# Layer A of a two-layer decoder trunk: order of the transposes and loads of x, the queue of the late loads, a fifth gate buffer, wider spreads, one block turned by TensorE

## The chip, the cores and the metric

The kernel runs on one core of one Trainium2 chip. The metric is device time in microseconds of one execution. The time before is 1515.4 us, the median of three runs (1513.81 to 1519.61). One execution was also recorded by the hardware profiler; it took 1514.66 us by its own count, and its span in the profile is 1512.9 us.

Engines are named as the profile names them: PE (TensorE matmuls), PEld (its weight loads), DVE (VectorE), ACT (ScalarE), POOL (GpSimd) and SP (the sync engine, which here starts transfers). A name with q at its end (SPq) is that engine's queue of instructions.

## The reference

Input `x` is 2048 rows of 1024 floats. Two layers follow each other. Only the first, layer A, is touched by the change:

```
h = rmsnorm(x, norm_g);  u = h @ w_in            # 1024 -> 2 x 1536
xb, gate = u[..., :1536], u[..., 1536:]
xb = causal_depthwise_conv(xb, conv_w, conv_b)   # 4 taps
r = sigmoid(xb_blocks @ wr + br);  i = sigmoid(xb_blocks @ wi + bi)   # 16 blocks of 96
log_a = -8 * r * softplus(-lam);   a = exp(log_a)
b = sqrt(-expm1(2 * log_a)) * (i * xb)
hs = linear recurrence h[s] = a[s] * h[s-1] + b[s]
x = x + (hs * silu(gate)) @ w_out                # 1536 -> 1024
```

Then K and V are made once from the new stream, and layer B is a sliding-window attention with 16 heads. All is float32 by the reference.

## The kernel before, in words

Every float32 operand of a product is split into two float16 parts, high and low, after it is scaled by a power of two. A product is then three float16 products (high-high, high-low, low-high: `PASSES`), added up in one PSUM bank. The power of two comes from the operand's largest magnitude: DVE takes maxima over each partition, `f2_turn` turns that column into a row with PE, `f2_round` takes the row's maximum and cuts it to a power of two on a small diagonal, and `f2_back` multiplies that by ones, which spreads the value over 128 partitions. This sequence is called a spread here (lines 231 to 249, `floor2_steps` from line 404).

Layer A works on units. The 2048 rows are 4 chunks of 512, the 1536 channels are 4 triples of 3 x 128; unit u is triple u // 4 at chunk u % 4, 16 units in all. For each unit PE makes the x-branch product `pu` (three banks, 72 matmuls of 512 columns), the gate product `pg` (72 more), and, while the next unit's `pu` runs, the small block product `pr` of the unit before. A unit's `pr` needs the convolution's result `xc`, its parts `hl` and a shared tile `b3` that is gathered with three small copies on SP (line 713). ACT, DVE and POOL carry the convolution, the sigmoids, the recurrence and the product with SiLU; POOL starts the store of the result to `yD` in DRAM (line 837). The SiLU's output lies in a ring of four buffers `gs`; a buffer is free when its store has landed.

The products need x normalized, split and transposed (`xnT`). Chunk 0 has four blocks of 128 rows: `first_norm` (line 897) makes the parts and `first_turn` (line 910) turns them, by PE with a copy out of PSUM for the blocks in `BY_PE`, and otherwise by a DMA transpose on SP (`flip`, line 330). `proj_first` (line 576) lets unit 0's first product run in groups of blocks (`FIRST`), as they come. Chunks 1 to 3 go through `ring_loads` and `norm_block` (three buffers in, three out) and `norm_flip`, which transposes both parts of a block in one DMA. The loads of these blocks and the transposes are both on SP.

Weights: triple 0 is prepared by `first_weights`, `first_others` and `first_gates`; triples 1 to 3 by `prep(g)` (line 535), which begins at a unit chosen by `PREP_AT` and loads through `Fetch` (three buffers `st`, started on SP). `w_out` (line 1120) loads the output weights twice, once for their maximum and once to split them. The first two output blocks of 128 rows follow directly behind unit 15 (`out_parts`, `out_products`), the others are written in plain order after that, with layer B's weight preparation between them.

The order of the instructions on each engine is fixed when the kernel is built. Each piece of work is a generator that names the engine and an estimated duration; `Plan` is a list scheduler that always takes the piece that can begin first by these estimates, with 30 ns per rank added as a handicap (`WEIGHT`, `RANKA`, `FIRST_RANK`). On the chip the engines run this order with semaphores, whatever the estimates were. `landing` estimates when a load arrives and keeps `plan.dma`, the time at which the loads issued so far are through.

Of the kernel before, what the change touches and what calls it, by code (L numbers as in the profile page):

```python
# [14 lines left out]
BF16 = mybir.dt.bfloat16  # L15
# [6 lines left out]
P = 128  # L22
# [44 lines left out]
RANKA = (1, 3, 1, 4, 2, 6, 1, 5, 6, 4, 10, 6, 4, 0)  # L67
FIRST_RANK = (2, 1, 5, 4, 3, 6, 5)
X_RING = (0, 1, 4)
# [116 lines left out]
def trunk(ctx, tc, x, wA, gw, par, gains, woA, wkv, wB, woB, vec, alib, out):  # L186
# [48 lines left out]
    def f2_round(tp, n):  # L235
        m1 = xp.tile([n, 1], F32, tag="f2m", name=uniq("f2m"), bufs=2)
        dve.tensor_reduce(m1, tp, AX.X, ALU.max)
        m2 = xp.tile([n, 1], F32, tag="f2n", name=uniq("f2n"), bufs=2)
        dve.tensor_scalar(m2, m1, 1e-30, None, ALU.max)
        m3 = xp.tile([n, 1], F32, tag="f2o", name=uniq("f2o"), bufs=2)  # L240
        dve.tensor_scalar(m3.bitcast(U32), m2.bitcast(U32), 0x7F800000, None, ALU.bitwise_and)
        dg = xp.tile([n, n], BF16, tag="f2d", name=uniq("f2d"), bufs=2)
        dve.tensor_scalar(dg, id32[:n, :n], m3, None, ALU.mult)
        return dg

    def f2_back(dg, n):
        bp = pst([P, n], F32, "tp", uniq("f2b"), TP_A)
        pe.matmul(bp, ones_b[:n, :], dg, start=True, stop=True)
        return bp
# [123 lines left out]
    def landing(kb):  # L373
# [3 lines left out]
        return t - plan.now  # L377

    def take_p1(tag, shape, dt=F32):
        f = yield from take(tag)  # L380
        return f, p1.tile(shape, dt, tag=tag, name=uniq(tag), bufs=BUFS[tag])

    class Fetch:


        def __init__(self, shape, src, rank):
            self.landed = flag()
            plan.go(self.steps(shape, src), rank)

        def steps(self, shape, src):  # L390
# [3 lines left out]
            nc.sync.dma_start(self.t, src)  # L394
            yield None, landing(P * shape[-1] * (shape[1] if len(shape) > 2 else 1) / 256)
            self.landed.set()
# [7 lines left out]
    def floor2_steps(mx, n, keep, slack=300):  # L404
        lock = yield from take("f2")
        free = yield from take("tp")
        if slack:
            yield None, slack
        yield PE_, 160
# [7 lines left out]
        yield PE_, 300  # L417
# [43 lines left out]

    def split_gates_steps(W, load, pw, rank):
        st = load.t
        yield DVE_, 200, 1
# [6 lines left out]
        for i in range(2):  # L471
            yield from split_steps(
                st[:, i * GCOLS : (i + 1) * GCOLS], sc, w[:, 0, i], w[:, 1, i], flag(), lo[i], 690, rank
            )
        W["gt"], W["pg"] = w, pw
        yield lo[1]
        load.free.set()
        W["gates"].set()
# [56 lines left out]
    def prep(g):  # L535
        W = WS[g]
        rank = RANKA[9]
        yield unit_f[4 * (g - 1) + PREP_AT[g - 1]]
        st = [Fetch([P, 4, 384], wsrc(g, 0, h), rank) for h in range(2)]
        sg = Fetch([P, 2 * GCOLS], gw[g], rank)  # L540
        m = col("m", 2)
# [5 lines left out]
        yield from split_part_steps(0, W, st, pw[:, 0:1], rank)  # L547
        st = [Fetch([P, 4, 384], wsrc(g, 1, h), rank) for h in range(2)]
        yield DVE_, 900, 1
        scales_x(g, W)  # L550
        yield from split_gates_steps(W, sg, pw[:, 1:2], rank)
        m = col("m")
# [281 lines left out]
    def store(un, j, t, gs):  # L834
# [5 lines left out]
        )  # L840
        yield None, 2600
        yield y_f[t][c]
# [17 lines left out]
    xfree = [flag() for _ in range(NB - 4)]  # L860
    hlfree = [flag() for _ in range(NB - 4)]
    x0free = [flag() for _ in range(CH // P)]
    par_f, decay_f = flag(), flag()
    w0_f, w0_st, w0_lo, px_f = [flag() for _ in range(4)], [], [flag() for _ in range(KD)], flag()

# [7 lines left out]
    def first_loads():  # L873
# [36 lines left out]
    def first_turn(b, w, src, fl):  # L910
        dest = xnV[0][:, w, :, b * P : (b + 1) * P]
        if b not in BY_PE:
            yield SP_, 1900
            flip(src, dest)
            yield None, 2500
        else:
# [3 lines left out]
            for k in range(KD):  # L920
                pe.transpose(tp[:, k], src[:, k * P : (k + 1) * P], id16)
            if w == 0:
# [21 lines left out]
    def first_weights():  # L944
# [14 lines left out]
        free = yield from take("tp")  # L959
        yield PE_, 300  # L960
        tot = pst([P, 1], F32, "tp", uniq("tot"), TP_A)
        pe.matmul(tot, ones, m0, start=True, stop=True)
        yield DVE_, 800, 1
        t = col("tot")
# [14 lines left out]
        for k in range(KD):  # L979
            if k < HI_DVE:  # L980
                yield DVE_, 320, 1
                dve.tensor_scalar(w[:, 0, k], w0_st[k // 4][:, k % 4], gs[:, k : k + 1], None, ALU.mult)
# [31 lines left out]
    def first_others(st):  # L1014
        W = WS[0]
        sg = Fetch([P, 2 * GCOLS], gw[0], FIRST_RANK[1])
        m = col("m", 2)
        yield from part_max_steps(st, m[:, 0:1])
        yield from gates_max_steps(sg, m[:, 1:2])
        pw = col("pw1", 2)  # L1020
        yield from floor2_steps(m, 2, pw)
        plan.go(first_gates(sg, pw), FIRST_RANK[3])
        yield from split_part_steps(1, W, st, pw[:, 0:1], FIRST_RANK[1])

    def first_gates(sg, pw):
        W = WS[0]
        yield from split_gates_steps(W, sg, pw[:, 1:2], FIRST_RANK[3])
        yield W["set1"]
        yield W["x"]
        yield DVE_, 180, 1  # L1030
        scales_g(W)
# [37 lines left out]
    def ring_loads():  # L1069
        for p in range(NB - 4):  # L1070
# [1068 lines left out]
```

## Time and profile before

| | before |
|---|---|
| median of three runs | 1515.4 us |
| profiled execution, its own time | 1514.66 us |
| its span | 1512.9 us |
| PE busy | 1485.0 us, 98% |
| DVE busy | 1015.9 us, 67% |
| ACT busy | 881.9 us, 58% |
| POOL busy | 412.4 us, 27% |
| mean granted clock of PE | 0.998 |

The table's shares are means over the span. Unit 0's first product begins at 13.48 us, unit 1 at 60.23 us, unit 15's gate product ends near 610 us, the first output product begins at 617.28 us; layer B's main part runs from about 870 us to the end. In a row of the timeline the first two numbers are start and length in us, "x8" is the number of instructions merged, and the bracket gives the idle time of the engine just before and what ended it. "issue" as a releaser means that the profile shows none.

### The profile page before, as it was taken

The page shows a single profiled execution, that of the slowest core. Times are in us where ns is not written, and L with a number is a line of the kernel's source. Part 1 is how long each engine was busy: PE and PEld are TensorE (multiplying, and loading weights), DVE is VectorE, ACT ScalarE, POOL GpSimd, SP SyncE. Part 2 cuts the span into 40 slices and gives each one's busy share as a digit, 9 for nine tenths or more (in the row PEclk, how much of TensorE's full clock was granted, in tenths as well). Part 3 has the DMA queues.
Part 4 walks back from the last instruction along what each step waited for, and adds up shares of the span by engine and source line. Part 5 has one row for each costly group of instructions (what it writes and reads, how often), then busy time and mean ns, then how long its engine had stood idle before and what let it go on. Part 6 is the DMA issues. An engine that isn't in the chain of part 4 may idle for free.

```text
span 1512.9 us, 23171 instructions
## 1 busy us (share of the span) xinstructions
PE 1485.0 (98%) x8572; PEld 734.4 (49%) x8572; DVE 1015.9 (67%) x2230; ACT 881.9 (58%) x1777; POOL 412.4 (27%) x548
## 2 busy tenths in 40 slices
PE   5999999999999999899999999999999999999998
PEld 4444444444444444344444455555555555555554
DVE  7877778778777766974147357656666665665686
ACT  5778667667666766601026157656665655655663
POOL 1232111111122111100000044444444444444531
PEclk9999999999999999999999999999999999999999
DMA  7863122022043313796338432444544444445531
GB/s 218 208 140 102 31 81 68 27 81 69 26 138 125 96 34 118 249 325 245 128 138 311 139 91 32 104 99 96 105 99 90 101 90 102 86 102 102 105 71 43
DMA packets 232210, 174.67 MB, mean 115 GB/s; under 512 B 194720, under 2 KB 205216, under 8 KB 232096
## 3 DMA queue, kind: packets, MB, share of 16 engines
q1 hardware_dynamic: 225808, 152.19, 38.2%
q0 software_dynamic: 6144, 20.98, 4.2%
q8 instruction: 67, 1.10, 0.3%
q14 instruction: 47, 0.39, 0.1%
q10 hardware_dynamic: 144, 0.01, 0.0%
HBM read 92.93 MB, written 29.36 MB: 81 GB/s over the span
## 4 chain that ended last, share of the span: by engine, by line
PE 94%; DMA 2%; DVE 2%; ACT 1%; issue 1%; SPq 0%; DVEq 0%; ACTq 0%
PE pm L286 35%; PE po L286 18%; PE pu L286 16%; PE pg L286 15%; PE pr L286 5%; PE s L286 3%; DMA xs<-in_x_dram 1%; DMA xnT<-in_wB_dram 0%; DMA xnT<-ri 0%; DVE wo L435 0%; PE tp L1697 0%; DMA qT<-qy 0%; DVE h L816 0%; DVE xnT L1194 0%; ACT ri L903 0%
## 5 line engine op out<-in xcount | busy, mean ns | idle before, releaser
L286 PEld LDWEIGHTS <-w 128*128 128x128 f16 x2448 | 234.3, 99 | 274.5 <-issue 10.0
L286 PE MATMUL pm<-wq,xT 128*128 128x512 f16 x1536 | 339.2, 379 | 0.0
L286 PEld LDWEIGHTS <-xT 128*128 128x128 f16 x1920 | 186.3, 98 | 177.3
L286 PE MATMUL pu<-xnT,w 128*128 128x512 f16 (+2 forms) x1296 | 261.1, 360 | 7.4 <-issue 3.2
L286 PE MATMUL po<-wo,xnT 128*128 128x512 f16 x1152 | 249.7, 379 | 4.2 <-DVE wo L435 2.4
L286 PE MATMUL pg<-xnT,w 128*128 128x512 f16 x1152 | 252.0, 379 | 0.0
L286 PEld LDWEIGHTS <-xnT 128*128 128x128 f16 x1152 | 112.5, 98 | 140.1 <-issue 5.2
L286 PE MATMUL pm<-xnT,yT 128*128 128x512 f16 x768 | 174.1, 379 | 0.3 <-ACT yT L1703 0.3
L694 DVE SCALAR_TENSOR_TENSOR xc<-u,cwS,xc 128x512 f32<-128x512 f32 x144 | 110.5, 781 | 52.4 <-ACT xc L690 49.7
L1909 ACT ACTIVATE sq<-sq,bi,ssc 128x128 f32<-128x128 f32 x256 | 124.0, 488 | 5.9 <-DVE bi L1906 5.6
L286 PEld LDWEIGHTS <-yT 128*128 128x128 f16 x768 | 73.1, 98 | 82.1 <-ACT yT L1703 0.4
L311 ACT ACTIVATE xnT<-xnT,sy 128x1536 f16<-128x1536 f32 x14 | 22.0, 1571 | 128.8 <-PE po L286 128.8
L1882 ACT COPY sq<-s 128x256 f32<-128x256 f32 x128 | 39.1, 383 | 96.5 <-PE s L286 96.3
L704 POOL TENSOR_TENSOR hl<-xc,hl 128x512 f16<-128x512 f32 x32 | 43.3, 1361 | 159.9 <-ACT hl L699 155.6
L675 ACT COPY u<-pu 128x512 f32<-128x512 f32 x48 | 27.8, 584 | 87.9 <-PE pu L286 87.7
L765 ACT ACTIVATE ri<-pr,pr,rsc 128x512 f32<-128x512 f32 x96 | 69.2, 779 | 5.2 <-PE pr L286 5.0
L837 POOL DMA_DIRECT2D yD<-gs x48 | 36.8, 767 | 119.1 <-DVE gs L827 118.8
L1283 DVE SCALAR_TENSOR_TENSOR xnT<-po,cA,xnT 128x512 f32<-128x512 f32 x28 | 20.8, 748 | 72.0 <-PE po L286 72.0
L1884 DVE COPY_PREDICATED sq<-mask,s 128x256 f32<-128x256 int32 x128 | 48.3, 437 | 28.0 <-ACT sq L1882 27.9
L286 PE MATMUL pr<-hl,gw 128*128 128x512 f16 x288 | 65.2, 379 | 0.0
L1893 DVE CUSTOM_DVE_ANT_0 sq<-sq,al 128x128 f32<-128x128 f32 x256 | 63.8, 297 | 0.0
L1837 POOL TENSOR_TENSOR rq<-qva,mhalf 128x16 f32<-128x16 f32 x16 | 49.6, 3100 | 44.6 <-DVE qva L1834 32.8
(277 smaller groups left out, 2193.3 us busy)
## 6 DMA issues: line engine op xcount, KB each, us to landing
xnT<-in_wB_dram SPq DMA_DIRECT2D x32, 512.0 KB, 6.1
yD<-gs POOLq DMA_DIRECT2D x48, 256.0 KB, 2.7
st<-in_woA_dram SPq DMA_DIRECT2D x24, 512.0 KB, 4.0
xnT<-yD SPq DMA_DIRECT2D x16, 768.0 KB, 5.2
st<-in_wA_dram SPq DMA_DIRECT2D x13, 768.0 KB, 6.2
xs<-in_x_dram SPq DMA_DIRECT2D x16, 512.0 KB, 4.3
xnT<-in_x_dram SPq DMA_DIRECT2D x16, 512.0 KB, 4.9
x1D<-xnT POOLq DMA_DIRECT2D x16, 512.0 KB, 4.2
```

Of the source, the lines that this page charges most:

```text
L286: lastmm[0] = pe.matmul(o, lhsT, rhs, start=start, stop=stop, skip_group_check=True)
L311: act.activation(hi, src, AF.Copy, scale=scale)
L675: act.copy(u[:, 3:], o)
L694: dve.scalar_tensor_tensor(xc, u[:, d : d + CH], cw[:, j, d : d + 1], xc, ALU.mult, ALU.add)
L704: (pool if j in LO_POOL else dve).tensor_tensor(hl[:, 1], xc, hl[:, 0], ALU.subtract)
L765: act.activation(v, o[j], AF.Sigmoid, bias=pr[:, t0 + j, 5 + w : 6 + w], scale=W["rsc"])
L837: pool.dma_start(yD[4 * c : 4 * c + 4, :, t, :].rearrange("b p n -> p b n"), gs.rearrange("p (b n) -> p b n", n=P),)
L1837: pool.tensor_tensor(rq, qva, mhalf, ALU.pow)
L1882: act.copy(sl, o[:, :, P:])
L1884: dve.copy_predicated(sl, mask.unsqueeze(1).to_broadcast([P, 2, P]), o[:, :, 0:P])
L1893: dve.tensor_tensor_reduce(s[:, h], s[:, h], al[:, i * P : (i + 1) * P], 1.0, -3.4e38, ALU.add, ALU.max, m)
L1909: act.activation(s[:, h], s[:, h], AF.Exp, bias=d["bi"][:, h : h + 1], scale=ssc[:, h : h + 1], accum_out=d["lsum"][:, h : h + 1],)
```

## The change

- `BY_PE = (0,)`: block 1 of chunk 0 is transposed by DMA as blocks 2 and 3 are; only block 0 is turned by PE. `FIRST = ((0, 2), (2, 4))`: the first product runs over two blocks at a time instead of one, two and one.
- `HI_DVE = 4`: DVE makes four of the first eight high weight parts instead of two, ACT the other four.
- The gate weights of triple 0 are loaded in `first_loads`, in two halves into two `gs` buffers, and are no longer a `Fetch` that waits for an `st` buffer.
- `ring_loads`: the load of block p (p >= 4) waits until the transpose of the last block of the chunk before has been issued.
- The plan's estimates of a transpose are smaller, plus the time until the loads issued before it are through (`behind_loads`).
- `Fetch` starts its loads on POOL by default; SP is kept for triples 0 and 1.
- `PREP_AT`: triples 1 and 2 begin a unit later, the output weights a unit earlier.
- `gs` has five buffers.
- The diagonal of a spread is a fixed tile of 128 partitions, zero outside the corner, and the spreading matmul runs over 128 partitions instead of n.
- New ranks. In particular the recurrence of units 14 and 15 gets `RANKA[13]` = 10 added, where it was 0.

```
-PREP_AT = (1, 1, 0, 3)
-FIRST = ((0, 1), (1, 3), (3, 4))
+PREP_AT = (2, 2, 0, 2)
+FIRST = ((0, 2), (2, 4))
...
-BY_PE = (0, 1)
-HI_DVE = 2
+BY_PE = (0,)
+HI_DVE = 4
+OUT_ACT = 0
...
-RANKA = (1, 3, 1, 4, 2, 6, 1, 5, 6, 4, 10, 6, 4, 0)
-FIRST_RANK = (2, 1, 5, 4, 3, 6, 5)
+RANKA = (2, 3, 1, 4, 1, 0, 0, 5, 4, 4, 10, 6, 3, 10)
+FIRST_RANK = (1, 0, 2, 2, 0, 6, 6)
...
+    diag = [cp.tile([P, 4], BF16, name=f"diag{i}") for i in range(2)]
+    for t in diag:
+        pool.memset(t, 0.0)
...
-        dg = xp.tile([n, n], BF16, tag="f2d", name=uniq("f2d"), bufs=2)
-        dve.tensor_scalar(dg, id32[:n, :n], m3, None, ALU.mult)
-        return dg
+        cnt[0] += 1
+        dg = diag[cnt[0] % 2]
+        dve.tensor_scalar(dg[:n, :n], id32[:n, :n], m3, None, ALU.mult)
+        return dg[:, :n]
...
-        pe.matmul(bp, ones_b[:n, :], dg, start=True, stop=True)
+        pe.matmul(bp, ones_b, dg, start=True, stop=True)
...
-    BUFS = dict(W=4, st=3, mm=MM_A, tp=TP_A, u=3, xc=4, hl=4, b3=2, gs=4, ri0=4, ri1=4, q=3, h=2, gw=2, f2=1)
+    BUFS = dict(W=4, st=3, mm=MM_A, tp=TP_A, u=3, xc=4, hl=4, b3=2, gs=5, ri0=4, ri1=4, q=3, h=2, gw=2, f2=1)
...
+    def behind_loads():
+
+        return max(plan.dma - max(plan.now, plan.free[SP_]), 0)
...
-            yield SP_, 450
+            yield queue, 450 if queue == SP_ else 750
             self.t = p1.tile(shape, F32, tag="st", name=uniq("st"), bufs=BUFS["st"])
-            nc.sync.dma_start(self.t, src)
+            (nc.sync if queue == SP_ else pool).dma_start(self.t, src)
...
+        queue = SP_ if g == 1 else POOL_
+        st = [Fetch([P, 4, 384], wsrc(g, 0, h), rank, queue) for h in range(2)]
+        sg = Fetch([P, 2 * GCOLS], gw[g], rank, queue)
...
-        plan.go(first_others([st3, Fetch([P, 4, 384], wsrc(0, 1, 1), 0)]), FIRST_RANK[1])
+        st = [st3, Fetch([P, 4, 384], wsrc(0, 1, 1), 0, SP_)]
+        for i in range(2):
+            f, t = yield from take_p1("gs", [P, CH])
+            yield SP_, 500
+            nc.sync.dma_start(t[:, 0:GCOLS], gw[0, :, i * GCOLS : (i + 1) * GCOLS])
+            plan.go(arrive(240, g0_f[i]), 0)
+            g0.append(t[:, 0:GCOLS])
+            g0_free.append(f)
+        plan.go(first_others(st), FIRST_RANK[1])
...
         if b not in BY_PE:
-            yield SP_, 1900
+            yield SP_, 1300 + behind_loads()
             flip(src, dest)
-            yield None, 2500
+            yield None, 2000
...
-        sg = Fetch([P, 2 * GCOLS], gw[0], FIRST_RANK[1])
...
+        mg = col("mg", 2)
+        for i in range(2):
+            yield g0_f[i]
+            yield DVE_, 640
+            dve.tensor_reduce(mg[:, i : i + 1], g0[i], AX.X, ALU.max, apply_absolute_value=True)
+        yield DVE_, 160
+        dve.tensor_reduce(m[:, 1:2], mg, AX.X, ALU.max)
...
                 yield xfree[p - 3]
+            if p >= 4:
+                yield turned_f[(p - 4) // 4 * 4 + 3]
             yield SP_, 450
...
-        yield SP_, 2000
+        yield SP_, 1400 + behind_loads()
         flip(t, xnV[c].rearrange("p w k n -> p (w k) n")[:, :, b * P : (b + 1) * P])
-        yield None, 3000
+        turned_f[p].set()
+        yield None, 2100
```

The halves of the gate weights reach `split_gates_steps` as two tiles with two flags to free them; other estimates in the plan change by a few tens of nanoseconds.

More of the change, by code (lines that the diff above doesn't have):

```diff
@@ L383, in trunk, with __init__, steps @@
     class Fetch:
-        def __init__(self, shape, src, rank):
+        def __init__(self, shape, src, rank, queue=POOL_):
             self.landed = flag()
-            plan.go(self.steps(shape, src), rank)
-        def steps(self, shape, src):
+            plan.go(self.steps(shape, src, queue), rank)
+        def steps(self, shape, src, queue):
             self.free = yield from take("st")
-            yield SP_, 450
+            yield queue, 450 if queue == SP_ else 750
             self.t = p1.tile(shape, F32, tag="st", name=uniq("st"), bufs=BUFS["st"])
-            nc.sync.dma_start(self.t, src)
+            (nc.sync if queue == SP_ else pool).dma_start(self.t, src)
             yield None, landing(P * shape[-1] * (shape[1] if len(shape) > 2 else 1) / 256)
@@ L408, in floor2_steps @@
             yield None, slack
-        yield PE_, 160
+        yield PE_, 110
         tp = f2_turn(mx, n)
@@ L416, in floor2_steps @@
             yield None, slack
-        yield PE_, 300
+        yield PE_, 40
         bp = f2_back(dg, n)
@@ L460, in split_part_steps, with split_gates_steps @@
             st[h].free.set()
-    def split_gates_steps(W, load, pw, rank):
-        st = load.t
+    def split_gates_steps(W, st, frees, pw, rank):
         yield DVE_, 200, 1
@@ L476, in split_gates_steps @@
         yield lo[1]
-        load.free.set()
+        for f in frees:
+            f.set()
         W["gates"].set()
@@ L538, in prep @@
         yield unit_f[4 * (g - 1) + PREP_AT[g - 1]]
-        st = [Fetch([P, 4, 384], wsrc(g, 0, h), rank) for h in range(2)]
-        sg = Fetch([P, 2 * GCOLS], gw[g], rank)
+        queue = SP_ if g == 1 else POOL_
+        st = [Fetch([P, 4, 384], wsrc(g, 0, h), rank, queue) for h in range(2)]
+        sg = Fetch([P, 2 * GCOLS], gw[g], rank, queue)
         m = col("m", 2)
@@ L547, in prep @@
         yield from split_part_steps(0, W, st, pw[:, 0:1], rank)
-        st = [Fetch([P, 4, 384], wsrc(g, 1, h), rank) for h in range(2)]
+        st = [Fetch([P, 4, 384], wsrc(g, 1, h), rank, queue) for h in range(2)]
         yield DVE_, 900, 1
         scales_x(g, W)
-        yield from split_gates_steps(W, sg, pw[:, 1:2], rank)
+        yield from split_gates_steps(W, [sg.t[:, i * GCOLS : (i + 1) * GCOLS] for i in range(2)], [sg.free], pw[:, 1:2], rank)
         m = col("m")
@@ L840, in store @@
         )
-        yield None, 2600
+        yield None, 3200
         yield y_f[t][c]
@@ L861, in trunk @@
     hlfree = [flag() for _ in range(NB - 4)]
+    turned_f = [flag() for _ in range(NB - 4)]
     x0free = [flag() for _ in range(CH // P)]
     par_f, decay_f = flag(), flag()
+    g0, g0_f, g0_free = [], [flag() for _ in range(2)], []
     w0_f, w0_st, w0_lo, px_f = [flag() for _ in range(4)], [], [flag() for _ in range(KD)], flag()
@@ L959, in first_weights @@
         free = yield from take("tp")
-        yield PE_, 300
+        yield PE_, 450
         tot = pst([P, 1], F32, "tp", uniq("tot"), TP_A)
         pe.matmul(tot, ones, m0, start=True, stop=True)
-        yield DVE_, 800, 1
+        yield DVE_, 850, 1
         t = col("tot")
@@ L1015, in first_others, with first_gates @@
         W = WS[0]
-        sg = Fetch([P, 2 * GCOLS], gw[0], FIRST_RANK[1])
         m = col("m", 2)
         yield from part_max_steps(st, m[:, 0:1])
-        yield from gates_max_steps(sg, m[:, 1:2])
+        mg = col("mg", 2)
[5 more added lines that the diff above has]
+        dve.tensor_reduce(m[:, 1:2], mg, AX.X, ALU.max)
         pw = col("pw1", 2)
         yield from floor2_steps(m, 2, pw)
-        plan.go(first_gates(sg, pw), FIRST_RANK[3])
+        plan.go(first_gates(pw), FIRST_RANK[3])
         yield from split_part_steps(1, W, st, pw[:, 0:1], FIRST_RANK[1])
-    def first_gates(sg, pw):
+    def first_gates(pw):
         W = WS[0]
-        yield from split_gates_steps(W, sg, pw[:, 1:2], FIRST_RANK[3])
+        yield from split_gates_steps(W, g0, g0_free, pw[:, 1:2], FIRST_RANK[3])
         yield W["set1"]
```

6 lines of the change are left out of this document (3 added, 3 removed).

## The prediction

> **What bounds the kernel now.** I read the span on the page, then the table of stretches, then the timeline of TensorE (PE) and of the SP queue where PE stands still. The columns of the table are length, then busy us (instructions) of PE, weight loads, VectorE (DVE), ScalarE (ACT), GpSimd (POOL), then granted clock, DMA share, GB/s.
>
> ```profile
> span 1512.9 us, 23171 instructions
> ```
> ```profile
> 0.00:13.50 13.50, 2.67 (x19) 2.07 (x20) 7.42 (x17) 7.58 (x10) 3.26 (x15) 1.00 0.89 318
> 13.50:24.40 10.90, 7.84 (x84) 6.68 (x85) 10.48 (x21) 7.40 (x12) 1.06 (x3) 1.00 0.81 200
> 24.40:32.00 7.60, 6.31 (x37) 4.35 (x36) 4.38 (x8) 2.24 (x4) 0.74 (x2) 0.55 0.63 157
> 41.30:60.20 18.90, 15.77 (x74) 6.87 (x71) 16.26 (x54) 14.82 (x22) 4.66 (x11) 1.00 1.01 224
> 97.20:573.20 476.00, 476.00 (x2353) 212.44 (x2352) 368.50 (x564) 325.88 (x470) 94.33 (x175) 1.00 0.26 77
> 573.20:617.30 44.10, 42.21 (x220) 18.67 (x219) 29.34 (x44) 30.82 (x40) 8.05 (x12) 1.00 0.42 130
> 617.30:640.20 22.90, 20.54 (x94) 9.12 (x94) 21.95 (x29) 17.02 (x21) 0.00 (x0) 1.00 0.79 288
> ```
>
> From 97.2 to 573.2 us PE is never idle and no edit removes a product, so that stretch can only stay or get worse. What can be won lies in two places. The first is everything before unit 1's products begin at 60.23: the two products of unit 0 are twice a 15.54 us stretch, yet they end at 57.08 and a gap of 3.15 follows.
>
> ```profile
> 57.08 3.15 issue
> 81.65 15.54 PE pg L286 x72
> 60.23 5.34 PE pu L286 x24
> ```
>
> The second is the end of layer A, where PE waits 1.89 us for a PSUM bank that the last SiLU frees, and 0.84 and 1.51 us for the low parts of the output weights.
>
> ```profile
> 616.54 0.69 ACT L755 ACTIVATE gs<-pg,gsc 128x512 f32<-128x512 f32 x1 [4.68 <-DMA yD<-gs]
> 617.28 12.68 PE L286 MATMUL po<-wo,xnT 128*128 128x512 f16 x58 [1.89 <-ACT gs L755]
> 618.00 1.53 SPq L394 DMA_DIRECT2D st<-in_woA_dram  x2
> 630.80 0.81 PE L286 MATMUL po<-wo,xnT 128*128 128x512 f16 x3 [0.84 <-DVE wo L435]
> 633.12 7.07 PE L286 MATMUL po<-wo,xnT 128*128 128x512 f16 x32 [1.51 <-DVE wo L435]
> ```
>
> **The change part by part: the first 40 us.** Block 1 of x is no longer turned by PE, and the first product now takes blocks 0 and 1 together, so it cannot begin before block 1's high part has come through a DMA transpose. The loads ahead of that transpose end here:
>
> ```profile
> 15.50:17.40 1.90, 1.90 (x20) 1.90 (x19) 1.83 (x4) 1.90 (x4) 0.00 (x0) 1.00 1.04 388
> 17.40:19.40 2.00, 1.99 (x31) 1.75 (x29) 1.93 (x3) 2.00 (x4) 0.73 (x2) 1.00 0.07 25
> 20.20 0.34 SPq L394 DMA_DIRECT2D st<-in_gw_dram  x1
> 20.63 4.45 SPq L332 DMA_TRANSPOSE xnT<-ri  x2
> 26.46 2.10 PE L286 MATMUL pu<-xnT,w 128*128 128x256 f16 x9 [1.29 <-DMA xnT<-ri]
> 28.56 3.50 PE L286 MATMUL pu<-xnT,w 128*128 128x256 f16 x18
> 32.10 2.14 PE L286 MATMUL pu<-xnT,w 128*128 128x256 f16 x18
> ```
> ```profile
> L332 SPq DMA_TRANSPOSE xnT<-xs x12: 1791/3484/4560, 41.7 to 118.7; - x12
> L332 SPq DMA_TRANSPOSE xnT<-ri x4: 1241/1293/3011, 20.6 to 30.9; - x4
> ```
>
> The unit's gate weights (480 KB, 0.49 MB) are now loaded with the others, at 388 GB/s 1.3 us more, so the loads end at 17.4 + 1.3 = 18.7. A transpose costs SP 1.24 us and its data serve PE 1.4 us after the issue ends (20.63 + 4.45 = 25.08, PE goes on at 26.46). First product: 18.7 + 1.24 + 1.4 = 21.3, where it was 13.48. The remaining five transposes at 1.27 bring the last at 27.7, or about 29.5 if one load of a later block stays between them; PE then still has the second pair of blocks to do, so this lies beside it. (The 13.48 is no loss by itself: half of the old PE time up to 26.46 is waiting.)
>
> From 21.3 PE has 15.5 us of product, the maxima's small matmuls (three spreads of two, at 0.10 each by a row further down) and the clock. The old run was granted 0.55 between 24.4 and 32.0: from 26.46 to 32.0 eighteen matmuls take 3.50 us where the next eighteen take 2.14. The new kernel idles from 11.5 to 21.3, so I charge the same spell, 5.5 us at half clock = 2.7 us; bounds 0 (the clock in the rows stood at 1.00 at 13.5 after an idle start) and 7.6 x 0.45 = 3.4. Sum: 21.3 + 15.5 + 0.6 + 2.7 = 40.1 for the first gate product, 1.0 before the old one (41.15, the row below).
>
> ```profile
> 41.15 2.75 PE L286 MATMUL pg<-xnT,w 128*128 128x512 f16 x12
> 54.01 0.52 SPq L867 DMA_DIRECT2D xs<-in_x_dram  x1
> 54.58 3.51 SPq L332 DMA_TRANSPOSE xnT<-xs  x1
> 50.93 1.28 DVE L1096 SCALAR_TENSOR_TENSOR xs<-xs,r 128x1024 f16<-128x1024 f32 x1 [0.29 <-ACT xs L1094]
> ```
>
> The Trainium skill has a rule for this clock ("TensorE: Matmul & The Clock Gate", Part 1): PE idle for a window falls to half rate, and about 3.4 us of steady work lift it. Taking 3.4 instead of the 5.5 of the trace, the loss would be 1.7 and the time 1.0 us better; the spell in the rows is longer, so the rows decide.
>
> The gate product's weights must not be late for 40.1. Their maxima stood behind the gate weights: DVE idled 3.2 of the 7.6 us from 24.4 (waiting for that load, then for PE's turns), and with the load issued before the transposes this goes. The other shifts are small: two more high parts on DVE (0.37 each), a copy of 0.68 less; ACT has two high parts and a 0.99 copy less. I cost them at nothing; DVE is 96% busy from 13.5 to 24.4, so without cover it is 0.1 to 0.7 us.
>
> **The gap at 57.08.** Unit 1 needs chunk 1 of x. Its last low part was done at 52.2, but the transpose was issued at 54.58 behind a load and the three transposes before it, each slowed to 3.3 to 3.8 us with a load ahead of it. New: loads of later blocks wait until the chunk's four transposes are issued. A transpose of this size with nothing ahead is the row's minimum, 1.79: ready at 52.2 + 1.8 + 1.4 to 2.0 = 55.4 to 56.0 even if DVE is no earlier. PE arrives at 40.1 + 15.7 = 55.8. So unit 1 starts at about 55.8: **4.4 us saved**, at most 7.1 (no half clock and DVE earlier), at least 0.
>
> What is queued next is unit 0's small gate product, at 55.8 + 5.3 = 61.1. The convolution that feeds it had its last copy to the shared tile issued at 61.84, landing 1.9 later, 63.7. It must come 2.6 us earlier; the 3.2 us of DVE idle pay for that, barely.
>
> ```profile
> 59.91 1.93 SPq L713 DMA_DIRECT2D b<-hl  x3
> DMA to landing us min/median/max: 1.9/1.9/8.0
> ```
>
> **The end of layer A.** The last SiLU waited for the fourth-last gate buffer, whose store was issued at 610.26 and landed; with five buffers it needs the one stored at 606.69, 3.6 us earlier.
>
> ```profile
> 606.69 0.78 POOL L837 DMA_DIRECT2D yD<-gs  x1 [5.36 <-DVE gs L827]
> 610.26 0.76 POOL L837 DMA_DIRECT2D yD<-gs  x1 [0.25 <-DVE gs L827]
> 613.24 3.54 DVE L1194 SCALAR_TENSOR_TENSOR xnT<-xnT,sy 128x1536 f16<-128x1536 f32 x2
> 613.92 1.48 PE L286 MATMUL pr<-b,gw 96*32 96x512 f16 x18
> 616.70 3.67 DVE L435 SCALAR_TENSOR_TENSOR wo<-st,swo,wo 128x1024 f16<-128x1024 f32 x3
> ```
>
> So the 1.89 goes; what is late next, the low part of y's first block, ends at 615.0 (the first of the two from 613.24), before PE's small product at 615.4. The 2.35 come from loads at 618.00 that waited for DVE's three low parts from 616.70; these had stood behind the recurrence of units 14 and 15. The new ranks put that recurrence level with them (0 + 10 against 10), so they may go first; I take half, 1.2. **End: 3.1 saved**, bounds 0 and 4.2.
>
> **The rest.** The spreads over 128 partitions replace a matmul that costs PE 0.10; eight of them after the start: at most 0.8, I take 0.3. Later starts for the next weights, and their loads on POOL, lie beside PE; 34 more starts (10 for the weights of triples 2 and 3, 24 for the output weights) at the store's 0.77 are 26 us on an engine that is busy 94 of 476. Covered; the price without cover is the fourth rival.
>
> ```profile
> 336.33 0.10 PE f2b L248
> ```
>
> Sum: 4.4 + 3.1 + 0.3 = 7.8. The profiled execution took 1514.66 by its own count, which is 0.74 under the median of 1515.4: 1506.9, and 1507.6 beside the median.
>
> **Rivals.** (1) *Everything is won*: PE keeps full clock, DVE is early, both stalls at the end and the spreads go: 7.1 + 4.2 + 0.8 = 12.1, **1503.3**. For it: DVE's idle time is in the rows. Against: the 0.55 row after a shorter idle. (2) *DVE becomes the bound at the start*: it is busy 31.1 of the 37.4 us in the three stretches from 13.5 that are shown, and if its waits only move, gate weights, chunk 1 and convolution all come when they did. Then unit 0's small product starts where it did and only the end is won: **1512.0**. (3) *The change does not do what it says*: transposes stay slow because the stores or shared-tile copies take the loads' place, and DVE, 96% busy from 617.3, gives the end's gain back: **1515**. (4) *Slower, through late weights of triple 2*. Its second half was split into high and low parts here, and first used at 338.26:
>
> ```profile
> 287.53 2.13 ACT L440 ACTIVATE w<-st,gs 128x384 f16<-128x384 f32 x4
> 294.92 0.61 ACT L440 ACTIVATE w<-st,gs 128x384 f16<-128x384 f32 x1
> 338.26 6.91 PE pg L286 x32
> ```
>
> Starting a unit later (476 us over 13 units, 36.6) the split ends at 295.5 + 36.6 = 332, 6 us ahead of its use. Its loads now wait in POOL's queue, in order with the subtractions and stores; each us beyond 6 is a us of PE. Beyond 14 the gains are eaten, and with 22 us late PE waits 16: 1515.4 + 16 - 7.8 = **1523.6**. For it: nothing behind a load that waits can pass it on POOL. Against: in that stretch POOL is busy only a fifth of the time, and a start takes 0.76 or 0.78 us in the rows even where DVE is busy.
>
> The Trainium skill speaks against the move ("SBUF — State Buffer", SBUF: two separate sides): POOL writes the descriptors itself and is locked out while DVE holds the port they share, 620 ns becoming 3100 there. By that rule the two loads that follow each other come some 5 us later, an estimate from that page, which leaves 1 us of the 6; I put rival 4 at 0.08 instead of 0.05 for it.
>
> **How the numbers follow.** Forecast 0.45, rival 1 0.22, rival 2 0.15, rival 3 0.10, rival 4 0.08. The likeliest gives 1507.6, its own range 1504 to 1511. A difference of 0.5% (7.6 us) is about what a measurement of this kernel tells from none; the line is at 1507.8, in the middle of the forecast, so half of it (0.23) with rival 1 makes faster 0.45; the other half with 2 and 3 makes same 0.47; slower 0.08. The range from 1502 to 1515 leaves out rival 4 and the tails.
>
> **What would show it.** Right: the first product near 21 us; transposes of x at 1.2 to 1.8 us each without loads between the four of a chunk; a spell of half clock after 21; no gap between the gate product of unit 0 and unit 1, which begins at 54 to 57; PE gapless to about 569; no wait for a SiLU before the first output product and less than 1.2 us for output weights. Wrong: the first product far from 21, unit 1 beginning after 59, PE waiting between 95 and 565, or new waits for y's parts or output weights after 605.

## The result, and the profile after

The changed kernel took 1505.86 us (median) where the kernel before took 1515.14 us, measured side by side: a ratio of 0.9935, 95% interval 0.992 to 0.995. The forecast was 1507.6 with a range of 1502 to 1515, so the time is inside the range and 1.7 us below the forecast. The prediction's chances (faster 0.45, same 0.47) had left it open on which side of its line at 1507.8 the time would fall. Below it turns out that two terms of the sum were wrong by about 2 us each, in opposite directions, and cancelled.

One profiled execution of the changed kernel ran more than twice as long, with every matmul slow, so all readings below come from a second profile of the same kernel. That execution took 1506.80 us by its own count; its page begins:

```profile
span 1505.1 us, 23004 instructions
PE 1479.1 (98%) x8484; PEld 730.5 (49%) x8484; DVE 1018.8 (68%) x2233; ACT 880.7 (59%) x1774; POOL 439.8 (29%) x584
```

The span is 7.8 us shorter than the 1512.9 before. (The medians differ by 9.3 us; the profiled execution is the longest of its four, which ran from 1504.98 to 1506.80, so 7.8 is on the low side.) To see where, the run is cut at four events that both kernels have: unit 1's first product, unit 15's first product, the first output product, and layer B's first product `pm`. The rows of before that the prediction doesn't show are these, first of the timeline of PE, then of the chain of waits:

```profile
573.14 5.34 PE L286 MATMUL pu<-xnT,w 128*128 128x512 f16 x24
```
```profile
869.40 25.52 PE pm L286 x140
```

And after, from the timeline of PE near the end of layer A, and from the chain:

```profile
569.57 4.48 PE L292 MATMUL pu<-xnT,w 128*128 128x512 f16 x20
...
611.76 48.51 PE L292 MATMUL po<-wo,xnT 128*128 128x512 f16 x224
...
690.93 2.33 PE L292 MATMUL po<-wo,xnT 128*128 128x512 f16 x10 [0.84 <-DVE xnT L318]
```
```profile
861.89 25.52 PE pm L292 x140
```

Unit 1 begins at 57.96 (a row below), where it began at 60.23. Each line of the table is the difference of two starts:

| stretch | before, us | after, us | won |
|---|---|---|---|
| start of the span to unit 1 | 60.23 | 57.96 | 2.27 |
| unit 1 to unit 15 | 512.91 | 511.61 | 1.30 |
| unit 15 to the first output product | 44.14 | 42.19 | 1.95 |
| output products, to layer B's first `pm` | 252.12 | 250.13 | 1.99 |
| layer B, to the end of the span | 643.5 | 643.2 | 0.3 |
| sum | 1512.9 | 1505.1 | 7.8 |

The table of stretches of the changed kernel (columns as in the prediction) shows the same from the side of the engines:

```profile
0.00:20.90 20.90, 2.65 (x18) 2.04 (x18) 14.27 (x25) 12.04 (x15) 5.08 (x19) 1.00 0.96 324
20.90:30.00 9.10, 7.32 (x35) 4.92 (x36) 6.72 (x19) 3.44 (x7) 0.74 (x2) 1.00 0.86 181
58.00:569.60 511.60, 511.60 (x2536) 228.91 (x2535) 397.92 (x622) 360.81 (x519) 126.63 (x224) 1.00 0.28 83
569.60:611.80 42.20, 42.08 (x220) 18.73 (x219) 27.22 (x41) 31.21 (x40) 7.99 (x14) 1.00 0.50 174
611.80:862.00 250.20, 249.36 (x1159) 112.98 (x1159) 134.44 (x158) 68.40 (x68) 14.17 (x25) 1.00 0.63 221
```

PE is busy for every one of the 511.6 us between unit 1 and unit 15, and idles 0.8 us in the whole stretch of the output products. What is left to win in layer A lies in the first 58 us. There PE has little to do for 20.9 us, while the DMA engines are busy 96% of the time, and then goes on like this (timeline of PE):

```profile
20.97 1.44 PE L292 MATMUL pu<-xnT,w 128*128 128x256 f16 x6 [8.38 <-DMA xnT<-ri]
...
24.12 2.74 PE L292 MATMUL pu<-xnT,w 128*128 128x256 f16 x12 [1.71 <-DVE w L1003]
26.86 2.77 PE L292 MATMUL pu<-xnT,w 128*128 128x256 f16 x12
...
29.50 1.68 PE L292 MATMUL pu<-xnT,w 128*128 128x256 f16 x12
31.13 7.70 PE L292 MATMUL pu<-xnT,w 128*128 128x256 f16 x69
...
42.29 2.75 PE L292 MATMUL pg<-xnT,w 128*128 128x512 f16 x12
...
57.96 2.32 PE L292 MATMUL pu<-xnT,w 128*128 128x512 f16 x10
```

Three things are to be seen. The first product begins at 20.97, 0.3 from the 21.3 of the prediction. A matmul of 256 columns takes 0.228 us (2.74 / 12) up to about 29.6 and 0.112 (7.70 / 69) from 31.13: half speed, although the clock column of the table says 1.00 for this stretch. And PE waits 1.71 us for a high part of the weights that DVE writes (line 1003), a wait in the middle of the product that the prediction didn't foresee (the kernel before waited 1.36 us for a high part too, but ahead of its first product at 13.48). The gate product follows at 42.29 and ends where unit 1 begins; the gap of 3.15 is gone.

### The profile page after: what moved, and what is told of

It is laid out like the page before. It is cut to its first block, busy times and chain, and to the rows that moved or that the text cites. A ratio compares the mean times of both kernels' runs of the same rounds, so it can differ in the third digit from the quotient of the medians.

```text
span 3182.0 us, 23004 instructions
## 1 busy us (share of the span) xinstructions
PE 3157.9 (99%) x8484; PEld 1126.8 (35%) x8484; DVE 1013.9 (32%) x2233; ACT 889.3 (28%) x1774; POOL 421.7 (13%) x584
## 4 chain that ended last, share of the span: by engine, by line
PE 99%; DVE 0%; DMA 0%; issue 0%; SPq 0%
PE pm L292 37%; PE po L292 20%; PE pg L292 17%; PE pu L292 17%; PE pr L292 6%; PE s L292 3%; PE tp L1726 0%; DMA st<-in_wA_dram 0%; DVE ri L927 0%; DVE amx L437 0%; PE f2t L237 0%; DVE w L1003 0%; DVE amx L973 0%; SPq L896 0%; DVE x L2074 0%
## 5 line engine op out<-in xcount | busy, mean ns | idle before, releaser
L292 PE MATMUL pm<-wq,xT 128*128 128x512 f16 x1536 | 726.8, 682 | 0.0
L292 PEld LDWEIGHTS <-w 128*128 128x128 f16 x2376 | 351.1, 149 | 729.4 <-issue 703.6
L292 PE MATMUL pu<-xnT,w 128*128 128x512 f16 (+1 forms) x1224 | 543.5, 652 | 10.0 <-DMA xnT<-ri 8.5
L292 PE MATMUL pg<-xnT,w 128*128 128x512 f16 x1152 | 541.9, 682 | 0.0
L292 PE MATMUL po<-wo,xnT 128*128 128x512 f16 x1152 | 538.7, 682 | 0.0
L292 PEld LDWEIGHTS <-xT 128*128 128x128 f16 x1920 | 283.1, 148 | 499.8 <-issue 465.2
L292 PE MATMUL pm<-xnT,yT 128*128 128x512 f16 x768 | 369.1, 681 | 0.0
L292 PE MATMUL pr<-hl,gw 128*128 128x512 f16 x288 | 138.4, 680 | 0.0
L292 PE MATMUL pm<-wk,xT 128*128 128x256 f16 x384 | 94.0, 447 | 0.0
L292 PE MATMUL s<-kT,qT 128*128 128x256 f16 (+1 forms) x512 | 92.1, 416 | 0.0
```

What stands on the lines that cost most here:

```text
L292: lastmm[0] = pe.matmul(o, lhsT, rhs, start=start, stop=stop, skip_group_check=True)
```

## The experiments

Three questions stood open: what the start is really bound by, how the end was won, and whether the parts that were costed at nothing cost nothing. All kernels below are the changed kernel with the edit that is shown. The medians of before, each taken on the same chip as the runs, were 1514.44 (the changed kernel again, four buffers, no late rank, loads between), 1514.58 (idle matmuls, four buffers without the late rank, narrow spreads, late loads on SP) and 1515.89 us (the other four). An interval of four runs is some 2 to 2.6 us to either side, so a difference of 1 or 2 us between two of these kernels is read from the traces and not from the medians. Each ratio is to the kernel before, with its 95% interval; the changed kernel's own is 0.9940.

### The changed kernel again

No edit; this is the run with the profile above.

> The changed kernel itself, for a profile at full clock and a second timing: 1505.9 us again. By the prediction's steps the first product begins near 21 us, unit 1 at 54 to 57 us (60.23 before), the first output product about 4.4 to 6.3 us earlier than 617.28, and the waits for output weights are under 1.2 us together.

Measured: 1506.18 us, 0.9940 [0.9925, 0.9955]. The gain stands, at 8.3 us against the medians of this chip.

### Four gate buffers

```
-    BUFS = dict(..., gs=5, ...)
+    BUFS = dict(..., gs=4, ...)
```

> The changed kernel with four gate buffers instead of five (the order is planned anew with that). If the fifth buffer removed the 1.89 us wait for the last SiLU, 1507.8 us (+1.9) and that wait is back before the first output product. If the new ranks had removed it, 1505.9.

Measured: 1515.66 us, 1.0006 [0.9997, 1.0016]. With this one number put back, the whole gain is gone: 9.5 us for a stall that was 1.89 us before. The timeline of this kernel shows why:

```profile
614.92 1.51 POOL L848 DMA_DIRECT2D yD<-gs  x2
617.80 0.69 ACT L766 ACTIVATE gs<-pg,gsc 128x512 f32<-128x512 f32 x1 [6.41 <-DMA yD<-gs]
618.54 41.70 PE L292 MATMUL po<-wo,xnT 128*128 128x512 f16 x180 [7.49 <-ACT gs L766]
```

The last SiLU waits for a store that begins only at 614.92, where the store of the kernel before began at 610.26. The store is late because the recurrence that makes its data is; and that one has a new rank, 10 instead of 0. The stall costs more than its own 7.49 us, since PE is slow behind it:

```profile
618.00:622.00 4.00, 3.46 (x9) 1.23 (x9) 3.57 (x8) 3.97 (x6) 0.00 (x0) 0.50 0.81 250
```

The granted clock is 0.50 in these four us, and the first 386 output products take 86.17 us where the same 386 take 83.47 in the run with four buffers and the old rank (two sections on): 2.7 us more. The two next runs separate the buffer from the rank.

### No late rank

The recurrence of units 14 and 15 gets its old rank.

```
-RANKA = (2, 3, 1, 4, 1, 0, 0, 5, 4, 4, 10, 6, 3, 10)
+RANKA = (2, 3, 1, 4, 1, 0, 0, 5, 4, 4, 10, 6, 3, 0)
```

> The changed kernel with 0 instead of 10 added to the rank of the recurrence of units 14 and 15. If that rank let the output weights go first, their waits (2.35 us before) come back: 1507.1 to 1508.3 us. If the loads begun by GpSimd removed them, 1505.9.

Measured: 1506.78 us, 0.9944 [0.9930, 0.9959], 0.6 us above the changed kernel and within its interval. The output weights are late again, as before the change:

```profile
626.24 34.05 PE L292 MATMUL po<-wo,xnT 128*128 128x512 f16 x157 [1.55 <-DVE wo L445]
```

So the rank does what the prediction said of it, in kind. PE waits 1.55 here where the changed kernel waits 0.84 for y's part at 690.93; the difference, 0.7, is about what the median shows.

### Four gate buffers and no late rank

```
-    BUFS = dict(..., gs=5, ...)
+    BUFS = dict(..., gs=4, ...)
-RANKA = (..., 10)
+RANKA = (..., 0)
```

> The changed kernel with four gate buffers and without the late rank of units 14 and 15. If the 9.5 us of the run with four buffers came from the two together (the recurrence put off, so that a buffer is freed late), this run loses only the old wait: 1508.0 to 1509.0 us. If the fifth buffer alone is worth 9 us, 1515 again.

Measured: 1508.51 us, 0.9953 [0.9938, 0.9968].

```profile
608.35 0.77 POOL L848 DMA_DIRECT2D yD<-gs  x1 [0.25 <-DVE gs L838]
614.77 25.41 PE L292 MATMUL po<-wo,xnT 128*128 128x512 f16 x117 [2.09 <-ACT gs L766]
```

The four kernels together are a table of two by two (medians, us):

| | rank 10 | rank 0 |
|---|---|---|
| five buffers | 1506.2 | 1506.8 |
| four buffers | 1515.7 | 1508.5 |

By itself the fifth buffer is worth 1.7 us (1508.5 - 1506.8), close to the stall of 1.89 that the prediction took away with it; the medians alone wouldn't tell this, but the wait of 2.09 for the SiLU is there with four buffers and gone with five. By itself the late rank costs 7.2 us (1515.7 - 1508.5): it moves the store from 608.35 to 614.92 and the last SiLU from 614.03 to 617.80, which is 3.8 us, and the slow clock behind the longer stall adds the 2.7. Only together do they work, because with five buffers the last SiLU needs the store before that one, which the rank leaves early. These are the rows of the changed kernel, POOL's and then ACT's:

```profile
604.52 0.77 POOL L848 DMA_DIRECT2D yD<-gs  x1 [1.45 <-DVE gs L838]
```
```profile
611.02 0.69 ACT L766 ACTIVATE gs<-pg,gsc 128x512 f32<-128x512 f32 x1 [0.99 <-DMA yD<-gs]
```

The fifth buffer is what makes the rank affordable; the prediction priced the two one by one and saw no such tie.

### Loads between the transposes

```
-            if p >= 4:
-                yield turned_f[(p - 4) // 4 * 4 + 3]
```

> The changed kernel without the wait that keeps the loads of later blocks out of a chunk's four transposes. If those loads made the 3.15 us gap before unit 1, unit 1 begins 2.5 to 4.4 us later and the time is 1508.4 to 1510.3 us. If unit 1 now starts early because DVE and ACT are earlier, the time stays within 1 us of 1505.9.

Measured: 1507.19 us, 0.9944 [0.9928, 0.9961]: 1.0 us above the changed kernel, too little for the intervals to tell, and less than expected. The chain and the waits of its PE do show the old stall, half as long as the gap of 3.15 was:

```profile
59.67 5.34 PE pu L292 x24
```
```profile
PE pu L292 <- DMA xnT<-xs: 1.6, 1, 1.6
```

In the changed kernel the transposes (line 338) take as long as the prediction said; the three times are shortest, median and longest in ns, where the medians of before were 3484 and 1293:

```profile
L338 SPq DMA_TRANSPOSE xnT<-xs x12: 1623/1718/3673, 38.8 to 117.0; - x12
L338 SPq DMA_TRANSPOSE xnT<-ri x6: 1260/1282/3581, 14.2 to 23.9; - x6
```

With the loads between them they are slow again:

```profile
L338 SPq DMA_TRANSPOSE xnT<-xs x12: 1601/3775/4812, 38.7 to 118.6; - x12
```

So holding the loads back halves the transposes and takes the wait of 1.6 away, but chunk 1 is only part of what unit 1 waits for: PE itself comes at 57.96.

### The clock: idle matmuls ahead of the first product

24 matmuls of 512 columns, whose result isn't used, are put into PE's idle time before the first product.

```
+    def warm_up():
+        yield x_hi[0]
+        free = yield from take("mm")
+        o = pst([P, CH], F32, "mm", uniq("warm"), BUFS["mm"])
+        yield PE_, 6000
+        for _ in range(24):
+            pe.matmul(o, id16, xnV[0][:, 0, 0:4, 0:P], start=True, stop=True, skip_group_check=True)
+        free.set()
```

> The changed kernel with 24 idle matmuls of 512 columns (their result is not used) on PE between the matmul of the first maximum and the first product, where PE stood still from 12.6 to 21.0 us. If PE's slow clock holds unit 0 back (42 matmuls of 256 columns at 0.23 us instead of 0.11 after 21.0), the gate product begins 3 to 4.5 us before 42.3, and unit 1 is then bound by the transposes of chunk 1, whose last was issued by 53.1 and lands near 55: 1502.5 to 1503.5 us. If the data of unit 0 come no earlier than PE takes them, the time stays at 1505.5 to 1506.5.

Measured: 1506.44 us, 0.9939 [0.9922, 0.9956]. Nothing is won: unit 1 begins 1.1 us earlier than in the changed kernel (56.86), and at the end PE waits 2.16 us for y's part and 0.32 for the last SiLU, where it was 0.84 in all.

```profile
12.69 7.54 PE L971 MATMUL warm<-xnT,id 128*128 128x512 f16 x24
...
24.38 2.74 PE L292 MATMUL pu<-xnT,w 128*128 128x256 f16 x12 [2.44 <-DVE w L1013]
...
41.19 2.75 PE L292 MATMUL pg<-xnT,w 128*128 128x512 f16 x12
```

The gate product comes 1.1 us earlier, not 3.9 (what the slow matmuls cost in the changed kernel, worked out further down), because the clock doesn't stay: PE arrives early, waits 2.44 us for the high part instead of 1.71, and the twelve matmuls behind that wait take the same 2.74 us as without the warming. This run also settles whether the slow matmuls are the clock. These are the stretches from 24 to 26 us, first with the idle matmuls, then in the changed kernel:

```profile
24.00:26.00 2.00, 1.62 (x8) 1.19 (x9) 1.90 (x5) 1.53 (x4) 0.00 (x0) 0.50 1.00 195
```
```profile
24.00:26.00 2.00, 1.88 (x9) 1.34 (x10) 1.64 (x5) 1.27 (x3) 0.00 (x0) 1.00 1.07 198
```

The matmuls have the same duration; one record of the clock says 0.50, the other 1.00. The changed kernel's PE therefore runs at half clock up to about 29.6 us, and its clock column doesn't show it. The prediction had used such a 1.00 "at 13.5 after an idle start" as a bound of nothing; that reading wasn't safe. The Trainium skill warns of this ("TensorE: Matmul & The Clock Gate", Part 1): it calls the trace's events of the clock unreliable on this chip. The two rows above agree.

### The first weights' high parts first

The 1.71 us wait is for a high part that DVE writes behind other work. These are the two rows of the changed kernel's timeline of DVE: the maximum of another weight part, and the high part that PE waits for, which comes 9.2 us after the second one (14.47).

```profile
15.99 1.75 DVE L437 TENSOR_REDUCE amx<-xs 128x4 f32<-128x1536 f32 x1
...
23.65 0.41 DVE L1003 TENSOR_SCALAR w<-st,gs 128x384 f16<-128x384 f32 x1
```

Between 14.47 and 23.65 stand two such maxima (the row at 15.99 is the first), three low parts of x at 1.28 and the gate weights' first maximum. Here the ranks of the first weights and of the others are exchanged.

```
-FIRST_RANK = (1, 0, 2, 2, 0, 6, 6)
+FIRST_RANK = (0, 1, 2, 2, 0, 6, 6)
```

> The changed kernel with the first two ranks of the start exchanged (the weights of the first product before the maxima of the second half). If PE's 1.7 us wait at 22.4 for a high part on DVE is only an effect of these ranks, it goes, the gate product begins 1 to 1.7 us before 42.3 and the time is 1504.5 to 1505.2. If the time lost there comes back later (second-half weights late for the gate product, chunk 1 late), 1506 or more.

Measured: 1524.78 us, 1.0063 [1.0048, 1.0078], slower than before the change.

```profile
38.97 15.70 PE L292 MATMUL pg<-xnT,w 128*128 128x512 f16 x72
61.27 7.76 PE L292 MATMUL pu<-xnT,w 128*128 128x512 f16 x24 [6.59 <-DMA xnT<-xs]
145.71 8.21 PE L292 MATMUL pu<-xnT,w 128*128 128x512 f16 x24 [8.77 <-DMA xnT<-xs]
```

The wait vanishes and the gate product begins 3.3 us earlier. But what was put behind is the work on chunk 1: unit 1 now waits 6.59 us for its transposes and begins 3.3 us later than in the changed kernel, and unit 3 waits another 8.77 for chunk 3. After both waits PE is slow again (24 matmuls take 7.76 and 8.21 us instead of 5.34). So this exchange doesn't win back the time of the first 42 us: it trades unit 1 for unit 0. Whether another order on DVE would serve both, no run here shows.

### Both: idle matmuls and the high parts first

The two edits above together; again the idle matmuls' result isn't used.

```
+        plan.go(warm_up(), 0)
-FIRST_RANK = (1, 0, 2, 2, 0, 6, 6)
+FIRST_RANK = (0, 1, 2, 2, 0, 6, 6)
```

> Both: idle matmuls on PE up to 20 us and the exchanged ranks. If slow clock and that wait together make unit 0 late, PE works at full clock from 21.0, the gate product begins at 37 to 38.5 and unit 1 is bound by chunk 1's transposes at 55 to 56: 1503 to 1504 us. If DVE's order was the reason and the clock falls again in a new wait, 1505 to 1506.5 as with the idle matmuls alone.

Measured: 1523.46 us, 1.0054 [1.0039, 1.0069]. The gate product begins at 38.17 and unit 1 at 60.50: unit 0 is early and unit 1 is late in the same way. PE wasn't at full speed here either: it waited 2.06 us for the first transpose behind the idle matmuls, the granted clock stood at 0.50 from 22 to 24 us, and the 18 products from 21.25 took 3.58 us where they took 3.70 without the idle matmuls. So what a fast PE at 21 us would be worth stays untested; the run shows that chunk 1 decides when unit 1 begins.

### Two blocks turned by PE, as before

Only this part of the change is undone: block 1 of chunk 0 is turned by PE again, and the first product runs in groups of one, two and one block.

```
-FIRST = ((0, 2), (2, 4))
+FIRST = ((0, 1), (1, 3), (3, 4))
-BY_PE = (0,)
+BY_PE = (0, 1)
```

> The changed kernel with blocks 0 and 1 turned by PE and three groups (one, two, one block) in the first product, as before. By the prediction's step the DMA transpose of block 1 and the pairs are worth 1.0 us at the gate product: 1507. If the earlier gate weights and the ranks did all of the start, 1506 or less, with the first product near 14 us again.

Measured: 1505.13 us, 0.9935 [0.9918, 0.9953], no worse than the change.

```profile
13.69 1.15 PE L292 MATMUL pu<-xnT,w 128*128 128x128 f16 x9 [1.36 <-DVE w L1003]
...
22.95 3.70 PE L292 MATMUL pu<-xnT,w 128*128 128x128 f16 x21 [5.77 <-DVE w L445]
```

PE begins at 13.69, waits later instead (5.77 us for a low part), and has its gate product at 40.48 and unit 1 at 56.15, a little before the earliest of the kernels here with the change's start (40.60 and 56.27). So no gain of the block by DMA shows, though the interval doesn't exclude one of 1 us. What the start won comes from the other edits: the faster transposes, worth 1.6 us by the wait of the run above with the loads between, and as further candidates the gate weights loaded earlier, the high parts on DVE and the new ranks, which weren't taken apart.

### Narrow spreads

The spreading matmul runs over n rows again instead of 128.

```
-        return dg[:, :n]
+        return dg[:n, :n]
-        pe.matmul(bp, ones_b, dg, start=True, stop=True)
+        pe.matmul(bp, ones_b[:n, :], dg, start=True, stop=True)
```

> The changed kernel with the spreading matmul over n partitions, as before. If a wide spread saves PE 0.20 us (0.10 for itself and 0.10 for the products behind it, as the two traces read), ten spreads behind the start give 1508.0 us (+2.0). If only its own 0.10 counts, or less, 1506.2 to 1507.0.

Measured: 1507.44 us, 0.9948 [0.9933, 0.9963], 1.3 us above the changed kernel; the intervals overlap, but the trace is sharper. In the timeline of PE, unit 1 and unit 15 begin here:

```profile
57.03 5.34 PE L292 MATMUL pu<-xnT,w 128*128 128x512 f16 x24
...
569.95 4.48 PE L292 MATMUL pu<-xnT,w 128*128 128x512 f16 x20
```

That is 512.92 us for the middle stretch, where before took 512.91 and the changed kernel 511.61. The other kernels here with wide spreads, the changed kernel's start and no stall of PE in this stretch take 511.60 or 511.61 too. Seven spreads stand in the stretch, so one is worth 1.31 / 7 = 0.19 us. The chain shows where: before, with the products on both sides of a spread,

```profile
334.60 1.73 PE pu L286 x8
...
336.43 1.83 PE pu L286 x8
```

the eight products behind the narrow matmul take 0.10 longer than the eight ahead of it, beside its own 0.10 at 336.33. After the change the matmul takes nothing that the chain can show, and 64 products follow at 0.216 each, the 1.73 / 8 of undisturbed ones:

```profile
333.32 1.73 PE pu L292 x8
...
336.77 0.00 PE f2b L254
336.77 13.83 PE pg L292 x64
```

In this section's run the same matmul takes 0.10 again, and the 39 products behind it 8.52 us where the changed kernel's take 8.44.

### Late loads on SP

All late loads are begun by SP again.

```
-        def __init__(self, shape, src, rank, queue=POOL_):
+        def __init__(self, shape, src, rank, queue=SP_):
...
-        queue = SP_ if g == 1 else POOL_
+        queue = SP_
```

> The changed kernel with all loads of weights begun by SP, as before. If they lie beside PE on either queue, 1505.5 to 1506.5 us. If the move to GpSimd took the loads of the output weights out of the way of SP's other transfers, their waits come back: 1507 to 1508.5.

Measured: 1506.31 us, 0.9943 [0.9928, 0.9957], the changed kernel's time to 0.1 us, and the stretch from unit 1 to unit 15 takes 511.61 us here too. No gain or cost of the move shows. In the changed kernel a start on POOL took (shortest, median, longest in ns):

```profile
L404 POOL DMA_DIRECT2D st<-in_woA_dram x24: 528/550/572, 404.5 to 605.3; - x24
L404 POOL DMA_DIRECT2D st<-in_wA_dram x8: 753/755/766, 240.7 to 363.4; - x8
```

The Trainium skill's rule that spoke against the move ("SBUF — State Buffer", SBUF: two separate sides; POOL locked out while DVE holds their port, 620 ns becoming 3100) shows no effect here: DVE is busy 78% of the middle stretch (397.92 of 511.60 us), and the longest of these 32 starts is 766 ns. Whether these DVE instructions hold that port, no run here shows.

### Triple 2 one unit later

The fourth rival's lever, pulled further: the preparation of triple 2 begins a unit later than the change has it.

```
-PREP_AT = (2, 2, 0, 2)
+PREP_AT = (2, 3, 0, 2)
```

> The changed kernel with the weights of triple 2 begun one more unit later (36.6 us). In the changed kernel their second half is split by 313.5 us and first used at about 335, 21 us later. If each us beyond that is a us of PE (the prediction's fourth rival), PE waits 10 to 16 us near 330: 1516 to 1522 us. If the plan moves these pieces up when they are due, less than 5 us: below 1511.

Measured: 1551.81 us, 1.0237 [1.0222, 1.0252]: 45.6 us slower than the changed kernel, almost three times the most that was expected. The timeline of PE, and POOL's:

```profile
368.51 0.37 PE L237 MATMUL f2t<-id,m 128*1 128x128 f32 x1 [31.54 <-DVE m L538]
```
```profile
307.14 0.77 POOL L404 DMA_DIRECT2D st<-in_wA_dram  x1
...
358.37 0.75 POOL L404 DMA_DIRECT2D st<-in_wA_dram  x1 [1.55 <-DVE w L445]
```

The loads from 307.14 on, the next ones at 321.23 and 329.50, are those of triple 3, which begins at unit 8: they took the three `st` buffers before triple 2's second half, which could be loaded only at 358.37. PE stands still for 31.54 us because the maximum's small matmul is next in its order, and unit 8's products are behind it. Waits of 3.49, 3.40, 1.86 and 0.96 us elsewhere and a granted clock of 0.50 at the end of the stall are part of the rest of the 45.6. The mechanism of the rival is real, and its price is far more than one us for one us; the changed kernel stands a unit away from it.

## Why the prediction was right, and where it was wrong

**What bounds the kernel: right.** The middle stretch had nothing to win but the spreads, and nearly all the rest came from the start and the end of layer A.

**First product at 21.3: right** (20.97), though not term by term. The transposes with nothing ahead did take 1.26 to 1.28, but the one that PE waits for was begun at 14.24, among the last loads, took SP 3.58 and landed 6.6 us after its issue, at 20.8. That the sum met it is in part luck.

**The clock, 2.7: right in kind, and its size varies.** The spell is there, and in the profiled execution four groups are slow: 6, 12, 12 and partly 12 matmuls took 1.44, 2.74, 2.77 and 1.68 us, 8.63 for 42, which at 0.112 would be 4.70. That is 3.9 lost, above the bound of 3.4, because that bound took the spell of before at its recorded length and clock, and the new spell is both longer and unrecorded. In the other kernels here with the same start the same 42 matmuls lost 2.4 to 4.0, so 2.7 is a fair size and this execution was near the upper end.

**"I cost them at nothing" for the high parts on DVE: failed.** The prediction itself gave 0.1 to 0.7 us without cover, by the sum of the instructions added. The wait is 1.71 (1.7 in every kernel here with the change's start, except behind the idle matmuls), and it is not a matter of 0.37 us each: the new order puts maxima and low parts of x ahead of the third high part. Sums of busy time said nothing of an order. With both terms, 20.97 + 15.5 + 3.9 + 1.7 = 42.1 for the gate product (the prediction's 0.6 for the spreads' small matmuls left out), measured 42.29, predicted 40.1.

**Block 1 by DMA: the 1.0 us credited to the first 40 us doesn't show.** In the profiled execution the gate product begins 1.1 us later than before the change (42.29 for 41.15), and with that part undone it begins at 40.48.

**Unit 1 at 55.8, 4.4 us won: mechanism right, size wrong.** No gap, and the product of unit 0 takes the 15.7 that was assumed, but all of it 2.2 later: 57.96, so 2.27 won: the closed gap gives 3.15 and a shorter stretch of the gate product 0.26, and its later begin takes 1.14 back. In the kernels whose first 60 us are the same unit 1 begins at 56.3 to 58.1, by how long the slow clock lasted and, in the latest, by a first product 1.1 us later, which makes 2.1 to 4.0. The held-back loads themselves are worth 1.0 us by the medians and 1.6 by the wait, less than the gap they closed, since PE is now the later one. Unit 0's small product then did not stall, as predicted.

**The end, 3.1 won: right, 3.4.** The 1.89 is gone. Of the 2.35 for output weights all is gone, and a new 0.84 for y's part has come, which the prediction had named as a sign of being wrong: 1.51 net, where half (1.2) was taken. That the two edits depend on each other wasn't seen: with the rank alone the changed kernel would be no faster than before.

**The spreads, 0.3 with at most 0.8: failed.** The step priced the matmul's own 0.10 and put that down as the most. The products behind it lose as much again, so it is 0.19 each, 1.3 us in the middle stretch alone. The rest of what the table has without another name, some 0.5 us among the output products (1.99 less the 1.51) and 0.3 in layer B, fits the spreads there, but that is only argued.

**Loads on POOL and later starts, costed at nothing: right.** PE is without a gap from 58.0 to 569.6.

**The rivals.** The first and second (full clock, DVE early; only the end is won) both failed: the truth lay between, at half of the start. The third failed, as the rows of the transposes show. The fourth named a real cliff, but its slack of 6 us was wrong. In the changed kernel the second half's split ends here (ACT), at 313.5, while unit 8's gate product begins at 335.0, eight products of 0.216 ahead of the spread at 336.77:

```profile
311.93 1.62 ACT L450 ACTIVATE w<-st,gs 128x384 f16<-128x384 f32 x3
```

Before, SP began the first of these loads here:

```profile
201.55 1.17 SPq L394 DMA_DIRECT2D st<-in_wA_dram  x2
```

That is a slack of some 21 us. The prediction carried the end of the split along with the start, a unit later; but loads that begin 39 us later (240.7 where it was 201.6) were through 18 us later (313.5 where it was 295.5), since the preparation had waited on its way and now waits less. And "each us beyond is a us of PE" was too cheap, by the last run.

**Why the time came out nonetheless.** Start 2.1 too high; end 0.3 too low; the rest (1.30 + 0.06 + 0.48 + 0.29) 1.8 too low: the sum of 7.8 was met because two errors cancelled, which is luck. With the start of another execution (2.1 to 4.0 won) the sum would have come out up to 1.7 us further from the forecast. The range was wide enough for either.

## What to carry to other kernels

A buffer and a priority can be worth little or harm alone and much together: ask which transfer frees the buffer that the last stage needs, and whether the priority moves that transfer. When work is moved to an engine that is nearly full, read the order of its instructions and not the sum of their times, for a high part of 0.4 us can stand behind nine us of other things. And a margin in time says little about what lies beyond it: where buffers are shared, being a little later can let the next consumer in first, and the loss is then its whole stay.

## What the runs showed of the hardware

- The clock record can say 1.00 while PE runs at half speed: 12 matmuls of 256 columns took 2.74 us at a recorded 1.00 and the same 2.74 at a recorded 0.50. The durations of equal matmuls are the surer sign.
- A stall of 7.49 us left the granted clock at 0.50 behind it, and the next 386 matmuls took 2.7 us longer for it. A gap of 3.16 us cost nothing of the kind (24 matmuls in 5.34 us behind it).
- After 7.54 us of dense matmuls the clock was lost again within 4.15 us (20.23 to 24.38) in which PE had 0.82 us of work.
- A matmul with one or two rows between full ones costs PE 0.19 us (1.31 us for seven), about half of it in the matmuls behind it; with all 128 rows it costs nothing that can be seen.
- The DMA transposes of x took SP 3.78 us each (median) while plain loads stood between them on the queue, and 1.72 in the same kernel with these held back.
